# Constant tables loaded on the weight queue, and a final residual step in halves with stores on two queues

## The chip, the cores and the metric

The kernel runs on one core of a Trainium2 chip. The metric is the device time of one execution in microseconds (us), the median of several runs. PE is the matmul engine, PEld its weight loads, DVE the vector engine, ACT the scalar engine, POOL the general engine, SP the sync engine. SP and ACT each issue DMA transfers from a queue of their own (SPq and ACTq in the profile).

## The reference

A decoder trunk of two layers on 256 positions of width 2048 (float32): layer 0 is RetNet retention, layer 1 block attention, each followed by a gated MLP with a causal convolution, with RMS norms ahead of each part and at the end. Cut to what the change touches:

```python
def rms_norm(x, g):
    y = x * lax.rsqrt(jnp.mean(x * x, axis=-1, keepdims=True) + RMS_EPS)
    return y * g

def retention_mixer(h, w_in, gn_gain, w_out):
    q, k, v, g = split(h @ w_in)
    q = rotary(q, pos)                      # cos and sin tables: "rope"
    k = rotary(k, pos) * dk ** -0.5
    inner = (q @ k.T) * decay               # decay table per head: "dec"
    ...

def reference(x, ...):
    for i in range(2):
        h = h + mixer(rms_norm(h, mix_norm[i]))
        h = h + conv_ffn(rms_norm(h, ffn_norm[i]), ...)
    return rms_norm(h, final_norm)
```

## The kernel before

All weights are streamed once from memory in units of 1 MB (`raw`, three buffers). A unit has two halves; each half is split by ACT and DVE into a high part `wh` (L163) and a low part `wl` (L164), each in three buffers, and three products of high and low parts (or two instructions that cover them) give a float32-like result. `panel_b` (L277, L279) has the weights as the stationary operand, `panel_a` (L225 to L227) the activations. A list of halves is run in order (`run`); the split stands two halves ahead of the matmuls, and the load of unit u+1 is asked for at the split of unit u. A raw buffer is free again when both halves of its unit have been split.

The residual stream is `h` (two row tiles t of 128 positions, 2048 columns). At the start `first_dmas` loads pieces of x (into `h`) and of units 0 and 1 in turn on SP; `issue_dma` loads unit 2 in two pieces with the last two pieces of x ahead of them (L124 to L127), and later units whole (L129). `x_T` transposes x on PE (L301) into `hT`, four blocks of 128 columns at a time; the four blocks 4 to 7 need the x piece that L141 asks for. ACT's queue loads the identity and the gains first. `consts` (L518) loads the rotation table `rope` (256 KB) and the decay table `dec` (1 MB) on ACT's queue; it is asked for behind the third half (L526). The instructions on an engine need not stand in the order of these calls: the library that builds the program puts them in order, an engine then runs them strictly in that order, and a DMA is issued when the engine's queue comes to it. `rope` is first used in `use_rope` (L427), `dec` in `ret_scores` (L482).

At the end `last_half` (L610) handles the last 512 columns of each t when their matmuls are done: the residual addition from PSUM (L613), the squares with their sum (L614, which is L318 in the profile), the product with the final gain (L616), the sum of four partial sums of squares (`ssq`, L619), the power on POOL (L621), four multiplications by the result (L626 on ACT for j = 1, L628 on DVE for the others), and four stores on SP (L629). For t = 1 nothing is left on PE to run beside it.

Of the kernel before, what the change touches and what calls it, by code (L numbers as in the profile page):

```python
# [10 lines left out]
F32 = mybir.dt.float32  # L11
F32R = mybir.dt.float32r
BF16 = mybir.dt.bfloat16
AF = mybir.ActivationFunctionType
ALU = mybir.AluOpType
AX = mybir.AxisListType

P = 128
D = 2048
S = 256  # L20
# [48 lines left out]
def build(tc, a, out):  # L69
    nc = tc.nc  # L70
    ctx = ExitStack()
    cst = ctx.enter_context(tc.tile_pool(name="cst", bufs=1))
# [4 lines left out]
    scr = ctx.enter_context(tc.tile_pool(name="scr", bufs=1))  # L77
# [3 lines left out]
    act, dve, pe = nc.scalar, nc.vector, nc.tensor  # L81

    x = a["x"].rearrange("b (t p) d -> p (b t) d", p=P)
    o = out.rearrange("b (t p) d -> p (b t) d", p=P)

    ident = cst.tile([P, P], F32, name="ident")
    h = cst.tile([P, 2, D], F32, name="h")
# [5 lines left out]
    cw = [cst.tile([P, 4, 2 * NFB], F32, name=f"cw{i}") for i in range(2)]  # L93
    ones = cst.tile([P, P], F32, name="ones")
    mhalf = cst.tile([P, 2], F32, name="mhalf")
    ssq = cst.tile([P, 2, 4], F32, name="ssq")
    rB = cst.tile([P, S], F32, name="rB")
    rBq = cst.tile([P, S], F32, name="rBq")

# [11 lines left out]
    raws, parts = {}, {}  # L111

    order = []

    def load_x(c0, c1):
        nc.sync.dma_start(h[:, :, c0 * P : c1 * P], x[:, :, c0 * P : c1 * P])

    def issue_dma(u):
        src, n = units[u]
        raws[u] = wraw.tile([P, 2048], F32, name="raw")  # L120
        dst = raws[u].rearrange("p (c n) -> p c n", n=n)
        if u == 2:

            load_x(8, 12)  # L124
            nc.sync.dma_start(dst[:, :4], src[:, :4])
            load_x(12, 16)
            nc.sync.dma_start(dst[:, 4:], src[:, 4:])  # L127
        else:
            nc.sync.dma_start(dst, src)  # L129

    def first_dmas():
        (src0, n), (src1, _) = units[:2]
        for u in range(2):
            raws[u] = wraw.tile([P, 2048], F32, name="raw")
        dst0, dst1 = (raws[u].rearrange("p (c n) -> p c n", n=n) for u in range(2))
        load_x(0, 2)
        nc.sync.dma_start(dst0[:, :2], src0[:, :2])
        load_x(2, 4)
        nc.sync.dma_start(dst0[:, 2:4], src0[:, 2:4])
        nc.sync.dma_start(dst1[:, :4], src1[:, :4])  # L140
        load_x(4, 8)  # L141
        nc.sync.dma_start(dst0[:, 4:], src0[:, 4:])
        nc.sync.dma_start(dst1[:, 4:], src1[:, 4:])
        state["dma"] = 2

    def issue_split(i):
        u, hf = order[i]
        if i == 0:
            first_dmas()
        while state["dma"] <= min(u + 1, len(units) - 1):  # L150
            issue_dma(state["dma"])
            state["dma"] += 1
        r = raws[u][:, hf * 1024 : (hf + 1) * 1024]
        wh = whi.tile([P, 1024], F32R, name="wh")
        wl = wlo.tile([P, 1024], F32R, name="wl")
        if i == 0:
            for j in range(2):
                sl = slice(j * 512, (j + 1) * 512)
                x_T(2 * j, 2)
                act.activation(wh[:, sl], r[:, sl], AF.Copy)  # L160
                dve.tensor_tensor(wl[:, sl], r[:, sl], wh[:, sl].bitcast(F32), op=ALU.subtract)
        else:
            act.activation(wh, r, AF.Copy)  # L163
            dve.tensor_tensor(wl, r, wh.bitcast(F32), op=ALU.subtract)  # L164
        n = units[u][1]
        parts[i] = (wh.rearrange("p (c n) -> p c n", n=n), wl.rearrange("p (c n) -> p c n", n=n))
# [4 lines left out]
    def after(n, fn):  # L171
        later.append([state["mm"] + n, fn])
# [140 lines left out]
    def x_T(c0, n):  # L313
        to_T(hT, c0, lambda t, c: h[:, t, (c0 + c) * P : (c0 + c + 1) * P], c0, n)

    def square_t(j, t):
        junk = scr.tile([P, 512], BF16, name="junk")
        act.activation(junk, h[:, t, j * 512 : (j + 1) * 512], AF.Square, accum_out=ssq[:, t, j : j + 1])  # L318

    def square(j):  # L320
        for t in range(2):
            square_t(j, t)

    def rstd(dst, src, mul, eps):
        v = sml.tile([P, 2], F32, name="v")
        dve.tensor_scalar(v, src, mul, eps, op0=ALU.mult, op1=ALU.add)
        nc.gpsimd.tensor_tensor(dst, v, mhalf, op=ALU.pow)
# [2 lines left out]

    def make_r():
        v = sml.tile([P, 2], F32, name="vs")
        dve.reduce_sum(v, ssq, axis=AX.X)
        r["r"] = sml.tile([P, 2], F32, name="r")
        rstd(r["r"], v, 1.0 / D, RMS_EPS)

    def make_rB(use):
        make_r()
        pt = paux.tile([P, 2, S], F32, name="aux")
        for t in range(2):  # L340
            d = scr.tile([P, P], F32, name="diag")
            dve.tensor_scalar(d, ident, r["r"][:, t : t + 1], None, op0=ALU.mult)
            pe.matmul(pt[:, 0, t * P : (t + 1) * P], lhsT=ones, rhs=d, start=True, stop=True)  # L343
        use(pt[:, 0, :])
# [21 lines left out]
    dma0 = nc.scalar.dma_start  # L366
# [12 lines left out]
    def taps_load():  # L379
        for i in range(2):  # L380
            dma0(cw[i], a["l_taps"][:, i])
# [26 lines left out]
    def open_(name, **kw):  # L408
        es = ExitStack()
        pools[name] = es  # L410
        return es
# [3 lines left out]
    ret = {}  # L415
    yT = [None]

    def ret_open():
        es = open_("ret")
        p1 = es.enter_context(tc.tile_pool(name="ret1", bufs=1))  # L420
        ret["p1"] = p1
        ret["rope"] = p1.tile([P, 2, S], F32, name="rope")
        ret["dec"] = p1.tile([P, RH, S], F32, name="dec")
        yT[0] = p1.tile([P, 2 * KC, 2 * S], F32R, name="yT")
# [90 lines left out]
    xT_h = [hT]  # L515

    def ret_begin():
        def consts():  # L518
            dma0(ret["rope"], a["c_rope"])
            dma0(ret["dec"], a["c_decay"])  # L520

        for i in (1, 2, 3):
            midway[2 * i - 1] = lambda i=i: x_T(4 * i, 4)
        for j in range(4):
            after(1 + j if j < 2 else 2 * j, lambda j=j: square(j))
        after(3, lambda: consts())  # L526
        after(6, lambda: make_rB(use_rope))
        after(9, lambda: taps_load())

    def ret_head(hd):  # L530
        def k_done(acc):
            ret_qk("k")(acc)
            after(4, lambda: ret_scores(hd))

        def v_done(acc):
            ret_v(acc)
            after(2, lambda: ret_pv(hd))
            after(4, lambda: ret_yT(hd))
            if hd == 0:
                after(5, lambda: bias_load())  # L540
                after(7, lambda: bias_table())

        q = panel_b(w_in, hd * RDK, xT_h, ret_qk("q"), before=ret_begin if hd == 0 else None)
        k = panel_b(w_in, D + hd * RDK, xT_h, k_done)
        if hd == 0:
            emit_pairs(q, k)
        else:
            emit(q + k)
        emit(panel_a(w_in, KC, 4 * D + hd * RDV, xT_h, ret_g))
        emit(panel_a(w_in, KC, 2 * D + hd * RDV, xT_h, v_done))  # L550

    ret_open()
    for hd in range(RH):
        ret_head(hd)

# [54 lines left out]
    def last_half(acc, t):  # L610

        hs = h[:, t, 3 * 512 :]
        dve.tensor_tensor(hs, acc, hs, op=ALU.add)  # L613
        square_t(3, t)  # L614
        hg = ffn["p1"].tile([P, 512], F32, name=f"hg{t}", tag=f"u{t}")
        dve.tensor_tensor(hg, hs, fin[3], op=ALU.mult)  # L616
        v = sml.tile([P, 1], F32, name="vf")
        rf = sml.tile([P, 1], F32, name="rf")
        dve.reduce_sum(v, ssq[:, t, :], axis=AX.X)  # L619
        dve.tensor_scalar(v, v, 1.0 / D, RMS_EPS, op0=ALU.mult, op1=ALU.add)  # L620
        nc.gpsimd.tensor_tensor(rf, v, mhalf[:, :1], op=ALU.pow)  # L621
        for j in range(4):
            sl = slice(j * 512, (j + 1) * 512)
            src = h[:, t, sl] if j < 3 else hg
            if j == 1:
                act.activation(h[:, t, sl], src, AF.Copy, scale=rf)  # L626
            else:
                dve.tensor_scalar(h[:, t, sl], src, rf, None, op0=ALU.mult)  # L628
            nc.sync.dma_start(o[:, t, sl], h[:, t, sl])  # L629

    def ffn_layer(layer, begin, g_next, use_next, last):
        wu, wd = a["ffn_w_up"][layer], a["ffn_w_down"][layer]
# [180 lines left out]
```

## Time and profile before

| | us |
|---|---|
| median of 3 runs | 2618.73 |
| lowest and highest of them | 2617.67, 2626.54 |
| profiled execution, its own time | 2617.12 |
| span of the profiled execution | 2615.1 |
| PE busy in the span | 2596.3 |

The span runs from the first to the last instruction of the profiled execution; 2.0 us of its time lie around it. PE is busy for 99% of the span. What is left is read at the two ends: the first 15 us, where x and the first weights arrive, and the 8 us behind the last matmul.

### The profile page before, as it was taken

Reading aid. Unit: us, or ns where it says so; the run is one execution under the profiler, and the core shown is the slowest. Engines: PE = TensorE matmul, PEld = TensorE weight load, DVE = VectorE, ACT = ScalarE, POOL = GpSimd, SP = SyncE. Lnnn points to the kernel's source line nnn. Section 1 sums busy time; section 2 is a strip of 40 time slices with the busy share of each in tenths; the row PEclk is TensorE's granted clock in tenths of the full one; section 3 lists DMA queues with packets and bytes.
Section 4 is the critical chain, followed back from the end, with each engine's and each line's share of the span. In section 5 each row is a group of like instructions: output and inputs, shape, how many; then the busy total and the mean of one; then the engine's idle time right before and its main releaser. Section 6 shows DMA issues by size and latency. Waiting matters only on the chain.

```text
span 2615.1 us, 33467 instructions
## 1 busy us (share of the span) xinstructions
PE 2596.3 (99%) x13482; PEld 2223.3 (85%) x13482; DVE 1664.2 (64%) x2087; ACT 1300.7 (50%) x1659; POOL 10.2 (0%) x24
## 2 busy tenths in 40 slices
PE   8999999999999999999999999999999999999998
PEld 7888888888888888888888888888888888888887
DVE  5666566565557777777555566665577777775454
ACT  5444444444445555555444454444555555554443
POOL 0000000000000000000000000000000000000000
PEclk9999999999999999999999999999999999999999
DMA  7655555555555565556555555555565555556554
GB/s 238 227 187 178 181 170 186 178 190 180 193 181 189 193 193 187 187 191 193 193 192 188 196 189 181 174 185 174 180 193 189 187 189 193 193 187 207 194 193 153
DMA packets 372410, 493.85 MB, mean 189 GB/s; under 512 B 8080, under 2 KB 258976, under 8 KB 372000
## 3 DMA queue, kind: packets, MB, share of 16 engines
q1 hardware_dynamic: 366224, 482.38, 56.4%
q10 hardware_dynamic: 6032, 9.35, 1.1%
q8 instruction: 105, 1.72, 0.3%
q14 instruction: 49, 0.40, 0.0%
HBM read 489.57 MB, written 5.27 MB: 189 GB/s over the span
## 4 chain that ended last, share of the span: by engine, by line
PE 99%; DMA 0%; issue 0%; DVE 0%; ACT 0%; POOLq 0%; POOL 0%; DVEq 0%
PE acc L277 34%; PE acc L279 17%; PE acc L225 15%; PE acc L227 15%; PE acc L226 15%; PE aux L301 1%; PE aux L292 1%; PE aux L293 1%; PE aux L291 1%; DMA h<-in_x_dram 0%; PE aux L735 0%; PE aux L343 0%; DVE wl L164 0%; ACT wh L163 0%; DVE h L628 0%
## 5 line engine op out<-in xcount | busy, mean ns | idle before, releaser
L164 DVE TENSOR_TENSOR wl<-raw,wh 128x1024 fp32r<-128x1024 f32 x911 | 1115.2, 1225 | 880.5 <-ACT wh L163 879.8
L163 ACT ACTIVATE wh<-raw 128x1024 fp32r<-128x1024 f32 x911 | 966.2, 1061 | 1206.3 <-PE acc L227 589.5
L277 PE MATMUL acc<-hT,wh 128*128 128x512 f32 x3840 | 1343.3, 394 | 0.0
L279 PE MATMUL acc<-hT,wl 128*128 128x256 f32 x3840 | 1076.3, 280 | 0.0
L277 PEld LDWEIGHTS acc<-hT,wh 128*128 128x128 f32 x3840 | 719.6, 187 | 161.0
L279 PEld LDWEIGHTS acc<-hT,wl 128*128 128x128 f32 x3840 | 726.2, 189 | 1.0
L225 PE MATMUL acc<-wh,actT 128*128 128x512 f32 x704 | 274.0, 389 | 0.0
L227 PE MATMUL acc<-wh,actT 128*128 128x512 f32 x704 | 274.0, 389 | 0.0
L226 PE MATMUL acc<-wl,actT 128*128 128x512 f32 x704 | 273.9, 389 | 0.0
L225 PE MATMUL acc<-wh,hT 128*128 128x512 f32 x640 | 251.0, 392 | 0.1
L226 PE MATMUL acc<-wl,hT 128*128 128x512 f32 x640 | 249.4, 390 | 0.0
L227 PE MATMUL acc<-wh,hT 128*128 128x512 f32 x640 | 249.3, 390 | 0.0
L225 PEld LDWEIGHTS acc<-wh,actT 128*128 128x128 f32 x704 | 132.2, 188 | 27.7 <-DVE h L350 0.2
L227 PEld LDWEIGHTS acc<-wh,actT 128*128 128x128 f32 x704 | 132.2, 188 | 27.3
L226 PEld LDWEIGHTS acc<-wl,actT 128*128 128x128 f32 x704 | 132.2, 188 | 27.2
L586 DVE SCALAR_TENSOR_TENSOR t<-u,cw,t 128x256 f32<-128x256 f32 x352 | 146.8, 479 | 0.0
L227 PEld LDWEIGHTS acc<-wh,hT 128*128 128x128 f32 x640 | 120.2, 188 | 25.3
L225 PEld LDWEIGHTS acc<-wh,hT 128*128 128x128 f32 x640 | 120.2, 188 | 24.5 <-DVE bs L432 0.4
L226 PEld LDWEIGHTS acc<-wl,hT 128*128 128x128 f32 x640 | 120.3, 188 | 23.7
L225 PE MATMUL acc<-wh,yT 128*128 128x512 f32 x256 | 99.9, 390 | 0.0
L227 PE MATMUL acc<-wh,yT 128*128 128x512 f32 x256 | 99.6, 389 | 0.0
L226 PE MATMUL acc<-wl,yT 128*128 128x512 f32 x256 | 99.6, 389 | 0.0
(130 smaller groups left out, 1461.2 us busy)
## 6 DMA issues: line engine op xcount, KB each, us to landing
raw<-in_ffn_w_up_dram SPq DMA_DIRECT2D x176, 1024.0 KB, 5.1
raw<-in_ret_w_in_dram SPq DMA_DIRECT2D x93, 1024.0 KB, 5.2
raw<-in_ffn_w_down_dram SPq DMA_DIRECT2D x88, 1024.0 KB, 5.1
raw<-in_moba_w_qkv_dram SPq DMA_DIRECT2D x48, 1024.0 KB, 5.2
raw<-in_ret_w_out_dram SPq DMA_DIRECT2D x32, 1024.0 KB, 5.0
raw<-in_moba_w_out_dram SPq DMA_DIRECT2D x16, 1024.0 KB, 5.0
skewD<-tblD ACTq DMA_DIRECT2D x1, 3072.0 KB, 13.2
raw<-in_ret_w_in_dram SPq DMA_DIRECT2D x5, 512.0 KB, 9.3
```

The costliest lines, as they stand in the source:

```text
L163: act.activation(wh, r, AF.Copy)
L164: dve.tensor_tensor(wl, r, wh.bitcast(F32), op=ALU.subtract)
L225: pe.matmul(acc, lhsT=xh, rhs=wh[:, c, :], start=(k == 0), stop=False)
L226: pe.matmul(acc, lhsT=xh, rhs=wl[:, c, :], start=False, stop=False)
L227: pe.matmul(acc, lhsT=xl, rhs=wh[:, c, :], start=False, stop=(k == nk - 1))
L277: pe.matmul(acc[:, b, :], lhsT=wh[:, c, b * P : (b + 1) * P], rhs=xt[:, k, :], start=(k == 0), stop=False)
L279: pe.matmul(acc[:, b, S:], lhsT=wl[:, c, b * P : (b + 1) * P], rhs=xt[:, k, :S], start=False, stop=(k == KC - 1))
L291: pe.matmul(dst, lhsT=lh, rhs=rh, start=start, stop=False)
L292: pe.matmul(dst, lhsT=lh, rhs=rl, start=False, stop=False)
L293: pe.matmul(dst, lhsT=ll, rhs=rh, start=False, stop=stop)
L301: pe.transpose(pt[:, i, t * P : (t + 1) * P], src(t, c0 + i), ident)
L586: dve.scalar_tensor_tensor(t[:, i, :], u[:, i, tap : tap + S], c[:, tap, b : b + 1], t[:, i, :], op0=ALU.mult, op1=ALU.add)
```

## The change

The two loads of `consts` leave ACT's queue. `rope` is now issued on SP right behind the load of unit 3, `dec` right behind that of unit 5. In `last_half` the residual addition and the squares are made in two pieces of 256 columns each; the sums of squares of the two pieces have columns of their own, so `ssq` has five columns per t instead of four, and `make_r` reads the first four. The store of j = 1 goes to ACT's queue, the other three stay on SP.

```diff
-    ssq = cst.tile([P, 2, 4], F32, name="ssq")
+    ssq = cst.tile([P, 2, 5], F32, name="ssq")
...
+    consts = {}
...
             nc.sync.dma_start(dst, src)
+        if u in consts:
+            consts[u]()
...
-        dve.reduce_sum(v, ssq, axis=AX.X)
+        dve.reduce_sum(v, ssq[:, :, :4], axis=AX.X)
...
-        def consts():
-            dma0(ret["rope"], a["c_rope"])
-            dma0(ret["dec"], a["c_decay"])
...
-        after(3, lambda: consts())
...
     ret_open()
+    consts[3] = lambda: nc.sync.dma_start(ret["rope"], a["c_rope"])
+    consts[5] = lambda: nc.sync.dma_start(ret["dec"], a["c_decay"])
...
-        dve.tensor_tensor(hs, acc, hs, op=ALU.add)
-        square_t(3, t)
+        for i in range(2):
+            sl = slice(i * S, (i + 1) * S)
+            dve.tensor_tensor(hs[:, sl], acc[:, sl], hs[:, sl], op=ALU.add)
+            junk = scr.tile([P, 512], BF16, name="junk")
+            act.activation(junk[:, :S], hs[:, sl], AF.Square, accum_out=ssq[:, t, 3 + i : 4 + i])
...
-            nc.sync.dma_start(o[:, t, sl], h[:, t, sl])
+            (dma0 if j == 1 else nc.sync.dma_start)(o[:, t, sl], h[:, t, sl])
```

## Rows read from the trace of the kernel before

**Rows 1.** The page: the span, and busy us, share and instructions per engine.

```profile
span 2615.1 us, 33467 instructions
PE 2596.3 (99%) x13482; PEld 2223.3 (85%) x13482; DVE 1664.2 (64%) x2087; ACT 1300.7 (50%) x1659; POOL 10.2 (0%) x24
```

**Rows 2.** Stretches, PE alone: stretch, us, PE busy (instructions), clock, DMA share, GB/s.

```profile
60.00:2600.00 2540.00, 2540.00 (x13198) 1.00 0.58 188
2606.90:2615.10 8.20, 0.02 (x1) 0.72 0.67 249
```

**Rows 3.** The chain that ended last, first 20 us: start, us, what.

```profile
0.74 3.62 DMA h<-in_x_dram
4.37 8.69 DMA h<-in_x_dram
13.10 1.76 PE aux L301 x7
```

**Rows 4.** Timeline, ACT's queue: start, us, line, operation.

```profile
1.80 0.41 ACTq L519 DMA_DIRECT2D rope<-in_c_rope_dram  x1
4.20 0.34 ACTq L520 DMA_DIRECT2D dec<-in_c_decay_dram  x1
```

**Rows 5.** DMA issues by line: count, KB each, us from issue to landing.

```profile
dec<-in_c_decay_dram ACTq DMA_DIRECT2D x1, 1024.0 KB, 7.7
```

**Rows 6.** Stretches of 2 us, columns as in group 2.

```profile
4.00:6.00 2.00, 1.09 (x4) 1.00 0.90 312
8.00:10.00 2.00, 0.57 (x2) 1.00 1.05 420
12.00:14.00 2.00, 0.90 (x4) 1.00 1.06 357
```

**Rows 7.** Unit 3: its issue on SP, its landing, and the split on ACT.

```profile
16.93 0.37 SPq L129 DMA_DIRECT2D raw<-in_ret_w_in_dram  x1
DMA to landing us min/median/max: 7.8/7.8/7.8
26.19 1.05 ACT L163 ACTIVATE wh<-raw 128x1024 fp32r<-128x1024 f32 x1
```

**Rows 8.** Timeline, DVE: the first uses of the two tables.

```profile
36.09 0.68 DVE L427 TENSOR_TENSOR rope<-rope,aux 128x512 f32<-128x512 f32 x1
53.56 0.42 DVE L482 TENSOR_TENSOR pf<-aux,dec 128x256 f32<-128x256 f32 x1
```

**Rows 9.** Timeline behind the last matmul, DVE and ACT.

```profile
2606.96 0.69 DVE L613 TENSOR_TENSOR h<-acc,h 128x512 f32<-128x512 f32 x1 [0.31 <-PE acc L227]
2607.75 0.63 ACT L318 ACTIVATE junk<-h 128x512 bf16<-128x512 f32 x1 [1.65 <-DVE h L613]
2608.28 0.18 ACT L318 ACTIVATION_READ_ACCUMULATOR junk<-h 128x1 f32 x1
2609.51 0.72 ACT L626 ACTIVATE h<-h,rf 128x512 f32<-128x512 f32 x1 [1.04 <-POOL rf L621]
2610.31 0.48 DVE L628 TENSOR_SCALAR h<-hg,rf 128x512 f32<-128x512 f32 x1
```

**Rows 10.** Timeline, SP: the first and the last two of the last four stores.

```profile
2610.03 0.33 SPq L629 DMA_DIRECT2D out_dram<-h  x1
2610.93 0.89 SPq L629 DMA_DIRECT2D out_dram<-h  x2
```

**Rows 11.** Timeline: operations of 128x256 on DVE and ACT.

```profile
42.41 0.42 DVE L444 TENSOR_TENSOR m<-m,m 128x256 f32<-128x256 f32 x1
5.62 0.84 ACT L304 ACTIVATE hT<-aux,gains 128x256 fp32r<-128x256 f32 x2 [2.39 <-PE aux L301]
```

**Rows 12.** The page: matmuls of one line with other operand tiles, count, busy us, mean ns.

```profile
L225 PE MATMUL acc<-wh,actT 128*128 128x512 f32 x704 | 274.0, 389 | 0.0
L225 PE MATMUL acc<-wh,hT 128*128 128x512 f32 x640 | 251.0, 392 | 0.1
```

**Rows 13.** The chain near the end, one step of the matmuls.

```profile
2600.12 0.23 PE acc L225
```

## The prediction

> **What bounds the kernel now.** I read the busy times first: PE works 2596.3 of the 2615.1 us [rows 1], so 18.8 us are idle. Next the stretches, to see where they lie: from 60 to 2600 us PE is never idle, and 8.2 us stand behind the last matmul [rows 2]. The rest, some 10.6 us, is the start. The change touches no matmul and no split, so it can gain only there, at most 18.8 us, and never all of it, since the first data must come and the last must go.
>
> Then the chain of waits at the start [rows 3]. It names one transfer: the piece of x for blocks 4 to 7, issued at 4.37 and landed at 13.06. PE waits for it until 13.10, transposes it, and from there has work until the end. So that landing sets the end of the whole kernel less the tail. The chain also shows that this issue at 4.37 came just as the first piece of x landed (0.74 + 3.62 = 4.36).
>
> What does this piece share the DMA engines with? ACT's queue issued rope at 1.80 and dec at 4.20 [rows 4], long before the calls' place in the code (behind the third half): the builder moved them forward. dec lands at 4.20 + 7.7 = 11.9 [rows 5], 1.2 us before the piece. The engines are full in this time: 312 to 420 GB/s with a busy share of 0.90 and above [rows 6]. So both tables, 1280 KB or 1.31 million bytes, are moved ahead of the piece that PE waits for.
>
> **The tables.** The change takes these 1.31 million bytes out from in front. At 420 GB/s, the rate while dec was moving, they took 3.1 us; at 357, the rate when SP alone was feeding, 3.7 us [rows 6]. The nearer row is hard to choose: the rate with dec in flight is the rate at which dec went, but what is left behind goes at SP's own. I take 3.4, so that the piece lands near 9.7. The lower bound is that SP alone ramps more slowly than both queues did: if the 5.3 us from the first piece's landing at 4.4 to 9.7 went at the 312 GB/s of the stretch from 4 to 6 us, not at the mean of the other two stretches, 389, they would take 1.3 us more. The gain lies between 2.1 and 3.7.
>
> The Trainium skill, "DMA: Bandwidth & Descriptors", section Specifications, gives some 358 GB/s as what HBM yields to one core. By that the tables would be worth 3.7 us and the sum would be 0.3 us lower. The trace went above it, at 420 GB/s over 2 us [rows 6], so the measured rate keeps its place.
>
> Does PE start 3.4 us sooner? The other loads of the start are on the same queue, behind or just ahead, and come forward by the same bytes, and the splits follow them. I count nothing for the matmuls' slow first steps: PE is idle ahead of them in either case.
>
> **Where the tables go.** On SP they stand among the weight loads: two more issues of 0.37 us [rows 7], on a queue that issues one unit about every five us; hidden. What they can delay is a unit behind them. Unit 3 was issued at 16.93 and landed 7.8 us later, at 24.7; its split ran at 26.19 [rows 7]. In the code rope stands behind unit 3, but as the builder moved it before, it may put rope, or both, ahead of unit 3, because that load waits for a buffer and the tables wait for nothing. With both ahead, unit 3 lands where it did, at 24.7, while its split could run at 22.8: up to 1.9 us late, part of which the split's lead of two halves takes up. Cost 0 as called, 0 to 1.9 otherwise; I take 0, since rope alone costs 0.7 us of transfer and the old margin was 1.5. The tables' users: rope at 36.09, dec at 53.56 on DVE [rows 8], some 33 and 50 after the shift. Had they come late, DVE, which runs in order, would hold the wl splits behind them, and PE behind those. rope lands near 22 and dec, behind unit 5, in the middle thirties at the latest: margins of 10 us.
>
> **The tail, squares.** Before, the addition starts at 2606.96 and takes 0.69, the square starts 0.10 behind its end, its sum is read 0.53 later and takes 0.18: done 1.50 after the start [rows 9]. In halves: the first addition ends at 0.42 [rows 11], the first square starts at 0.52. A square of 256 columns, from the operation of that size on ACT (0.42 each) [rows 11], hands over to the read of its sum after some 0.32; then 0.18 for the read, 0.03 to the next: the second square starts at 1.05 (its addition is done by 0.85), its sum is read from 1.37 and done at 1.55 to 1.57. That is 0.07 later than before: the second read of a sum eats what the overlap gives. Bounds: 0.2 us sooner, if the two squares overlapped fully, 0.3 later. The gain product (L616) moves by as little and hides beside the squares. For t = 0 the same happens beside matmuls and costs nothing.
>
> **The tail, stores.** Four stores on SP begin at 2610.03 and the last ends its issue at 2611.82, 0.43 to 0.47 each [rows 10]. The data of the last is ready at 2610.79 [rows 9], so SP's issuing is late, not the data. With three on SP, beginning 0.07 later: 2610.10, 2610.53, 2611.00, done 2611.40. ACT's multiplication ends at 2610.23 [rows 9], so its store is issued by some 2610.8, before SP's last. The 3.3 us from the last issue to the span's end stay. Net of both tail edits -0.4; bounds -0.7 to +0.3 (nothing, if what lands last isn't the last issued, with the squares' worst). For t = 0, ACT's store issue ends before ACT's next square; nothing waits.
>
> **The sum.** 2617.12 of the profiled execution, less 3.4, less 0.4: 2613.3. The median of the runs stands 1.6 above that execution, so the same sum on the median is 2614.9. I forecast 2614.2 between them. Against 2618.73 that is 0.17% faster, within the 0.5% that a measurement of this kernel can tell from no change.
>
> **The rivals.**
> The tables still stand in front. If the builder moves them on SP ahead of the x pieces, the piece for blocks 4 to 7 lands as before, and only the tail's 0.4 is left: 2616.7, on the median's footing 2618.3. For it: rope did move ahead by three halves. Against it: the x pieces wait for nothing either and were called first. 8%.
>
> Half of the gain is held elsewhere: unit 3 late by up to 1.9 us, or the splits on ACT and DVE become the chain. 2617.12 - 1.5 - 0.4 = 2615.2. For it: the margin of 1.5 us [rows 7]. 12%.
>
> More is gained: in the gap of PE ahead of 13.10 there could be matmuls of the first half, if the builder orders them ahead of the transposes. Up to 2 us more: 2611.3. 8%.
>
> Slower: ssq grows from 32 to 40 bytes in each partition, and tiles allocated behind it may lie at other addresses. If a matmul's read of 512 columns then touched one more memory line of four float32 columns, at 0.23 us for 512 columns [rows 13] that is 1.8 ns for each of 13482 matmuls [rows 1], 24 us in all: 2613.3 + 24.3 = 2638. It decides from 0.28 ns per matmul on, which eats the 3.8 us. Against it: matmuls of one line that read actT and hT, which lie at different places, take 389 and 392 ns [rows 12]; the trace shows no addresses, so those two may share an alignment. 4%. The Trainium skill, "SBUF — State Buffer", section Specifications (TRN2), speaks for this rival: it says that the memory has lines of 16 bytes and that each crossing to a new line costs. No row of this trace shows such a price.
>
> **How the numbers follow.** The forecast has 68%: startup 2.1 to 3.7, tail -0.7 to +0.3, on either footing 2612.7 to 2616.9. The range goes below to the case of more gain and above to that of no gain at the start on the median's footing, with part of the scatter of the runs: 2610.8 to 2619.2. Faster by over 0.5% would take 13 us out of 18.8 idle: 1%. Slower by over 0.5% comes only from the moved tiles: 3%. Else the same: 96%.
>
> **What would show it.** Right: the chain's transfer of x lands near 9.7 instead of 13.06, PE's transposes start there, PE is idle some 3.4 us less and has no new gap up to 60 us; behind the last matmul there are two reads of sums and the power on POOL starts no sooner; SP issues three stores and ends some 0.4 us nearer to the last matmul, and ACT's store is issued in between. Wrong: rope or dec issued before the second piece of unit 2, a wait of ACT for unit 3, or a matmul mean that moved by a nanosecond or more.

## The result: 0.76% slower, and where the time went

| | before | after |
|---|---|---|
| median of 5 runs, us | 2618.40 | 2639.49 |
| lowest and highest, us | 2617.67, 2626.54 | 2639.45, 2641.22 |
| profiled execution, own time, us | 2617.12 | 2639.49 |
| its span, us | 2615.1 | 2637.7 |

The ratio is 1.0076, 95% interval 1.0062 to 1.0090. The forecast was 2614.2 (2610.8 to 2619.2), so the result lies outside the range, at the rival that had 4%. Some executions of the kernel before, and of those that place their tiles like it, run one stretch of the up projections at 236 ns per `wh` matmul instead of 230, 9 us more in all (2627 instead of 2618); where a profile below is such an execution, the text says so.

Lines of the code have moved: L277 and L279 are now L280 and L282, L225 to L227 are L228 to L230, L129 is L130, L301 is L304, L613 is L615, the squares of the tail (L318) are L617, L621 is L624 and L629 is L632.

The page of the kernel after, busy times (against [rows 1]):

```profile
span 2637.7 us, 33475 instructions
...
PE 2623.5 (99%) x13482; PEld 2225.6 (84%) x13482; DVE 1665.7 (63%) x2089; ACT 1301.5 (49%) x1663; POOL 10.2 (0%) x24
```

PE is busy 27.2 us longer with the same 13,482 matmuls, and idle 14.2 us instead of 18.8. So the change won 4.6 us of idle time, as it was meant to, and lost 27.2 us inside the matmuls.

The steady stretch of the kernel after, PE alone (columns as in [rows 2]):

```profile
60.00:2600.00 2540.00, 2540.00 (x13079) 1.00 0.57 187
```

PE has no gap here in either kernel and the granted clock is 1.00 in both, but 119 fewer matmuls fit in than in [rows 2]. At 0.227 us each (a step of the kind in [rows 13]) these are 27.0 us.

Which matmuls grew (line, operands, count, busy us, mean ns of one): first two groups of the kernel before, then the page of the kernel after.

```profile
L277 PE MATMUL acc<-hT,wh 128*128 128x512 f32 x3840 | 1343.3, 394 | 0.0
L279 PE MATMUL acc<-hT,wl 128*128 128x256 f32 x3840 | 1076.3, 280 | 0.0
```

```profile
L280 PE MATMUL acc<-hT,wh 128*128 128x512 f32 x3840 | 1359.8, 397 | 0.0
L282 PE MATMUL acc<-hT,wl 128*128 128x256 f32 x3840 | 1080.9, 281 | 0.0
...
L228 PE MATMUL acc<-wh,actT 128*128 128x512 f32 x704 | 274.1, 390 | 0.0
...
L228 PE MATMUL acc<-wh,hT 128*128 128x512 f32 x640 | 254.2, 397 | 0.1
...
L228 PE MATMUL acc<-wh,yT 128*128 128x512 f32 x256 | 99.9, 390 | 0.0
```

In [rows 12] `wh,actT` stood at 389 and `wh,hT` at 392. Now every group that reads `hT` is longer, and no other by more than 1 ns: `hT,wh` went from 394 to 397, `hT,wl` from 280 to 281, `wh,hT` from 392 to 397. These means include the overlap of one matmul with the next; what counts is the step from start to start. The timeline of PE around 2000 us (start, us, what), first before:

```profile
2000.13 0.39 PE L277 MATMUL acc<-hT,wh 128*128 128x512 f32 x1
2000.36 0.28 PE L279 MATMUL acc<-hT,wl 128*128 128x256 f32 x1
2000.48 0.39 PE L277 MATMUL acc<-hT,wh 128*128 128x512 f32 x1
2000.71 0.28 PE L279 MATMUL acc<-hT,wl 128*128 128x256 f32 x1
2000.83 0.39 PE L277 MATMUL acc<-hT,wh 128*128 128x512 f32 x1
```

and after:

```profile
2000.04 0.40 PE L280 MATMUL acc<-hT,wh 128*128 128x512 f32 x1
2000.28 0.28 PE L282 MATMUL acc<-hT,wl 128*128 128x256 f32 x1
2000.40 0.39 PE L280 MATMUL acc<-hT,wh 128*128 128x512 f32 x1
2000.63 0.28 PE L282 MATMUL acc<-hT,wl 128*128 128x256 f32 x1
2000.74 0.40 PE L280 MATMUL acc<-hT,wh 128*128 128x512 f32 x1
```

Before, the step behind a `wh` matmul is 0.23; after, it alternates 0.24 and 0.23. Worked out from all start times of the up projections, it grew from 230 to 234.6 ns, and the one behind `wl` from 116.7 to 118.7; in `panel_a` the steps that read `hT` grew from 227 to 233.5, and those that read `actT` or `yT` stayed at 227.

Aligning the two traces matmul by matmul gives the account. (The first 141 stand in another order, so up to there the matmuls are only counted.) At the 50th matmul the kernel after is 4.80 us ahead, from there to the last it loses 27.34, and the tail adds under 0.1. Together 22.6, the difference of the spans. The two up projections of the MLPs are 18.5 of the 27.3: each takes 482.0 us before and 491.2 after.

**Where the tiles lie.** The program as built gives the start of every tile in the partition, in bytes. In it a tile takes a multiple of 32 bytes, so `ssq` takes 32 before (4 x 2 floats) and 64 after (5 x 2 floats, 40 bytes), and every tile allocated behind it moves by 32.

| tile | before | after |
|---|---|---|
| hT | 33472 | 33472 |
| wh | 96704 | 96736 |
| wl | 108992 | 109024 |
| actT, oT (one place) | 123584 | 123616 |
| yT | 133824 | 133856 |

Before, any two of these differ by a multiple of 256 bytes (wh less hT is 63232, 247 times 256; actT less wh is 26880, 105 times). After, `hT` alone is 32 off from the others, and the matmuls that grew are those with `hT`.

### The profile page after: what moved, and what is told of

Its sections match the earlier page's. It is cut to its first block, busy times and chain, and to the rows that moved or that the text cites. A ratio compares the mean times of both kernels' runs of the same rounds, so it can differ in the third digit from the quotient of the medians.

```text
span 2637.7 us, 33475 instructions
## 1 busy us (share of the span) xinstructions
PE 2623.5 (99%) x13482; PEld 2225.6 (84%) x13482; DVE 1665.7 (63%) x2089; ACT 1301.5 (49%) x1663; POOL 10.2 (0%) x24
## 4 chain that ended last, share of the span: by engine, by line
PE 99%; DMA 0%; issue 0%; DVE 0%; ACT 0%; SPq 0%; POOLq 0%; POOL 0%; DVEq 0%
PE acc L280 34%; PE acc L282 17%; PE acc L228 15%; PE acc L229 15%; PE acc L230 15%; PE aux L304 1%; PE aux L296 1%; PE aux L295 1%; PE aux L294 1%; DMA h<-in_x_dram 0%; PE aux L738 0%; PE aux L346 0%; DVE wl L167 0%; ACT wh L166 0%; ACT junk L617 0%
## 5 line engine op out<-in xcount | busy, mean ns | idle before, releaser
L280 PE MATMUL acc<-hT,wh 128*128 128x512 f32 x3840 | 1359.8, 397 | 0.0
L282 PE MATMUL acc<-hT,wl 128*128 128x256 f32 x3840 | 1080.9, 281 | 0.0
L280 PEld LDWEIGHTS acc<-hT,wh 128*128 128x128 f32 x3840 | 721.7, 188 | 174.5 <-DVE hT L310 0.2
L282 PEld LDWEIGHTS acc<-hT,wl 128*128 128x128 f32 x3840 | 724.6, 189 | 1.0
L228 PE MATMUL acc<-wh,actT 128*128 128x512 f32 x704 | 274.1, 390 | 0.0
L230 PE MATMUL acc<-wh,actT 128*128 128x512 f32 x704 | 273.9, 389 | 0.0
L228 PE MATMUL acc<-wh,hT 128*128 128x512 f32 x640 | 254.2, 397 | 0.1
L230 PE MATMUL acc<-wh,hT 128*128 128x512 f32 x640 | 252.6, 395 | 0.0
L228 PEld LDWEIGHTS acc<-wh,actT 128*128 128x128 f32 x704 | 132.2, 188 | 27.6 <-DVE h L353 0.2
L230 PEld LDWEIGHTS acc<-wh,actT 128*128 128x128 f32 x704 | 132.2, 188 | 27.5
L229 PEld LDWEIGHTS acc<-wl,actT 128*128 128x128 f32 x704 | 132.2, 188 | 27.3
L230 PEld LDWEIGHTS acc<-wh,hT 128*128 128x128 f32 x640 | 120.0, 187 | 29.2
L228 PEld LDWEIGHTS acc<-wh,hT 128*128 128x128 f32 x640 | 120.0, 188 | 28.1 <-DVE bs L435 0.4
L228 PE MATMUL acc<-wh,yT 128*128 128x512 f32 x256 | 99.9, 390 | 0.0
L230 PE MATMUL acc<-wh,yT 128*128 128x512 f32 x256 | 99.7, 389 | 0.0
```

Source lines behind the costliest of these rows:

```text
L228: pe.matmul(acc, lhsT=xh, rhs=wh[:, c, :], start=(k == 0), stop=False)
L229: pe.matmul(acc, lhsT=xh, rhs=wl[:, c, :], start=False, stop=False)
L230: pe.matmul(acc, lhsT=xl, rhs=wh[:, c, :], start=False, stop=(k == nk - 1))
L280: pe.matmul(acc[:, b, :], lhsT=wh[:, c, b * P : (b + 1) * P], rhs=xt[:, k, :], start=(k == 0), stop=False)
L282: pe.matmul(acc[:, b, S:], lhsT=wl[:, c, b * P : (b + 1) * P], rhs=xt[:, k, :S], start=False, stop=(k == KC - 1))
```

## Experiments: does the place of the tiles cost the 27 us?

The first theory is that the time follows from where a matmul's operands lie relative to each other. The rivals are that the 27 us come from the moved loads, or from the code of the tail. "Steady" below is what a kernel loses against the one before between the 50th and the last matmul, from traces aligned as above.

**e1.** The kernel before, with 32 unused bytes behind `ssq`; no instruction differs.

```diff
     ssq = cst.tile([P, 2, 4], F32, name="ssq")
+    cst.tile([P, 8], F32, name="pad0")
```

> The kernel before, with an unused tile of 32 bytes behind ssq, so that all tiles behind it (raw, wh, wl, actT and the rest, not hT) lie 32 bytes higher; no instruction is other than before. Theory P (the place of the weight parts against hT is what the matmuls pay for): steps of the matmuls with hT grow as in the changed kernel, 27 us in all, 2645 us. Rival Q (the other order of loads, the halves or the two queues slow it): 2618 us, as before. Rival C (the place makes no difference): 2618 us.

Measured: 2645.05 against 2618.36, ratio 1.0097 (1.0079 to 1.0115); steady +27.33, where the kernel after had +27.34. Its matmuls by line:

```profile
L277 PE MATMUL acc<-hT,wh 128*128 128x512 f32 x3840 | 1359.3, 397 | 0.0
L279 PE MATMUL acc<-hT,wl 128*128 128x256 f32 x3840 | 1080.7, 281 | 0.0
```

The same 397 and 281 as after. An unused tile costs the whole loss.

**e3.** The kernel after, its `mhalf` and `ssq` in one tile of 64 bytes, so that all else lies as before.

```diff
-    mhalf = cst.tile([P, 2], F32, name="mhalf")
-    ssq = cst.tile([P, 2, 5], F32, name="ssq")
+    misc = cst.tile([P, 16], F32, name="misc"); mhalf = misc[:, 10:12]
+    ssq = misc[:, :10].rearrange("p (t j) -> p t j", t=2)
```

> The changed kernel with mhalf and ssq in one tile of 64 bytes, so that every tile behind them lies where it lay in the kernel before. All instructions of the change are there. Theory P: 2618.4 less the 4.8 us by which the matmuls of the changed kernel start sooner, 2613 to 2614 us, steps of the matmuls with hT as before. Rival Q: 2639 us.

Measured: 2612.87 against 2618.36, ratio 0.9986 (0.9971 to 1.0001). At the 50th matmul it is 4.70 us ahead, and 0.1 is lost from there to the 8000th; behind that its profiled execution (2621.62) is one at 236 ns. All that the change does, without the 32 bytes, is worth 5.5 us by the medians, which the interval, with executions at both levels in it, can't tell from no change; the aligned trace shows the 4.7. The 32 bytes cost 26.6 (2639.49 less 2612.87).

**e4.** The kernel before, with an unused tile ahead of `hT` grown by 32 bytes, so that all operands move together.

```diff
-    cst.tile([P, 16], F32, name="gap0")
+    cst.tile([P, 24], F32, name="gap0")
```

> The kernel before with the unused tile ahead of hT 32 bytes larger, so that hT and all behind it lie 32 bytes higher together. Theory P in its relative form (hT against wh and wl): no change, 2618 us. Its absolute form (wh, wl at a place that is no multiple of 64 bytes): 2645 us, and then the matmuls with actT would be slower too, which they were not in the changed kernel.

Measured: 2616.12 against 2618.36, ratio 0.9984 (0.9972 to 0.9996); steady -1.9, the `hT,wh` group 393. It is the place of the operands relative to each other that costs; this one move of all together was worth 2 us, in the other direction. One of its ten executions took 3705.29 us, for which nothing here gives a reason; the others took 2615.3 to 2616.7.

**e2, e10, e9.** How the cost depends on the distance. e2 is the kernel after with 32 bytes more (64 in all); e10 and e9 are the kernel before with 128 and 256 unused bytes behind `ssq`.

```diff
+    cst.tile([P, 8], F32, name="pad0")      # e2, on the kernel after
...
+    cst.tile([P, 32], F32, name="pad0")     # e10
...
+    cst.tile([P, 64], F32, name="pad0")     # e9
```

> The changed kernel with 32 unused bytes more behind ssq, so that all behind it lies 64 bytes higher than in the kernel before. Theory P: if the pattern repeats with 64 bytes, the 27 us go and the gain of the start stays, 2612 us; if it repeats with more, something between 2612 and 2640. Rival Q: 2639 us, as the changed kernel.

> The kernel before, with 128 unused bytes behind ssq. 0 and 256 bytes gave 2618 us, 32 gave 2645, 64 gave 17 us over what the start and tail leave. If the pattern repeats with 128 bytes: 2618. If 256 is the period and half of it is as far as one can be from it: over 2630.

> The kernel before, with 256 unused bytes behind ssq. In the kernel before the places of hT and of wh, wl, actT, yT and oT differ by whole multiples of 256 bytes; 32 bytes off cost 27 us, 64 bytes off 22 us. If the pattern repeats with 256 bytes (or fewer, down to 128): 2618 us. If it needs more: over 2630 us.

| distance added, bytes | ratio, interval | steady, us | ns of hT,wh / hT,wl / wh,hT |
|---|---|---|---|
| 0 (before) | 1 | 0 | 394 / 280 / 392 |
| 32 (e1) | 1.0097 (1.0079 to 1.0115) | +27.3 | 397 / 281 / 397 |
| 64 (e2) | 1.0058 (1.0040 to 1.0076) | +22.3 | 398 / 281 / 393 |
| 128 (e10) | 1.0076 (1.0061 to 1.0091) | +20.0 | 395 / 283 / 397 |
| 256 (e9) | 0.9998 (0.9989 to 1.0008) | 0.0 | 394 / 280 / 392 |

e2 has the start's gain of the change in its ratio, the others have not. A period of 64 or of 128 bytes falls; 256 brings the time back. At the distances tried below it (none lies between 128 and 256) the cost is 20 to 27 us, and it moves between the kinds of matmul. The Trainium skill, "SBUF — State Buffer", section Specifications (TRN2), says that the memory has lines of 16 bytes and that each crossing to a new line costs. Shifts of 32, 64 and 128 bytes are whole lines and change no crossing, and they cost 27, 22 and 20 us: the measurement shows another effect than that rule.

**e5.** The kernel before, with `actT`, `oT` and `yT` moved by 32 bytes, and `hT`, `wh`, `wl` left.

```diff
     scr = ctx.enter_context(tc.tile_pool(name="scr", bufs=1))
+    scr.tile([P, 8], F32, name="pad0")
```

> The kernel before, with 32 unused bytes behind wl: hT, wh and wl lie where they lay, while actT, yT and oT, the other operands of the matmuls with wh and wl, lie 32 bytes higher. Theory P (it is the place of one operand against the other): now the matmuls with hT keep their steps and those with actT, yT and oT, 3264 of 128x512 in panel_a, go from 227 to 233 or so: 2618.4 + 3264 x 6.5 ns = 2639.6 us. Rival H (something is particular to hT or to its neighbours): 2618 us.

Measured: 2638.05 against 2618.13, ratio 1.0076 (1.0059 to 1.0093); steady +20.1. Its matmuls by line:

```profile
L277 PE MATMUL acc<-hT,wh 128*128 128x512 f32 x3840 | 1343.3, 394 | 0.0
...
L225 PE MATMUL acc<-wh,actT 128*128 128x512 f32 x704 | 278.5, 396 | 0.0
...
L225 PE MATMUL acc<-wh,hT 128*128 128x512 f32 x640 | 250.9, 392 | 0.1
```

Now the `hT` groups stay at 394 and 392, and `actT` goes from 389 to 396 (its step from 227 to 233.3 ns). The cost went to the pairs whose distance changed. So no tile is special; the distance is.

**e6 and e15: which two reads meet?** While a matmul streams its moving operand, the stationary operand of the next one is loaded (PEld is busy for 84% of the span beside PE's 99%). In `panel_b`, `hT` streams, and `wh` and `wl` are loaded in turn. Either the matmul's own two operands matter, or the stream and the load of the *next* weights. e6 moves `wl` and all behind it by 32; e15 moves `wh` alone by 32, and what lies behind it by 256.

```diff
+    ctx.enter_context(tc.tile_pool(name="padp", bufs=1)).tile([P, 8], F32, name="pad0")    # e6
     wlo = ctx.enter_context(tc.tile_pool(name="wlo", bufs=3))
...
+    ctx.enter_context(tc.tile_pool(name="pada", bufs=1)).tile([P, 8], F32, name="pad0")    # e15
     whi = ctx.enter_context(tc.tile_pool(name="whi", bufs=3))
+    ctx.enter_context(tc.tile_pool(name="padb", bufs=1)).tile([P, 56], F32, name="pad1")   # e15
     wlo = ctx.enter_context(tc.tile_pool(name="wlo", bufs=3))
```

> The kernel before, with 32 unused bytes between wh and wl: hT and wh lie where they lay, wl and all behind it 32 bytes higher. While one matmul streams its columns the weights of the next are loaded. Theory N (the streamed operand meets the load of the next weights): in panel_b the matmul with wh has the load of wl beside it and gets slower, the one with wl has the load of wh beside it and keeps its 117 ns. Theory O (a matmul's own two operands): the other way round, the step of the matmul with wl grows. Either way some 2630 to 2650 us; without an effect, 2618.

> The kernel before with wh 32 bytes higher, and wl and all behind it 256 bytes higher, so that only wh is off the common place; the mirror image of the run in which only wl and what lies behind it was. Theory N (the streamed operand meets the load of the next weights): in the second layer's up projection the step of the matmul with wl, which has the load of wh beside it, grows from 117 to 119 or more, and that of the matmul with wh stays near 230 or falls. Theory O (a matmul's own two operands): the step of the matmul with wh grows to 234 or more, that with wl stays at 117. Median by either some 2625 to 2645 us.

Measured: e6 2641.59 against 2618.13, ratio 1.0090 (1.0075 to 1.0105), steady +23.3; e15 2650.51 against 2626.95 (the kernel before ran mostly at 236 ns in that set), ratio 1.0095 (1.0077 to 1.0113), steady +34.6.

The two theories were to be told apart by the steps in the up projections. In e6 the step behind a `wh` matmul grew from 230 to 232 ns, and the one behind `wl` fell from 116.7 to 115. That is no cost: a pair takes 347 ns as before, only the start of the `wl` matmul in it has moved. The number of matmuls in 400 us of an up projection says the same (columns as in [rows 2]; in order, the kernel before, e6, e15 and the kernel after):

```profile
1950.00:2350.00 400.00, 400.00 (x2310) 1.00 0.59 190
1950.00:2350.00 400.00, 400.00 (x2310) 1.00 0.58 190
1950.00:2350.00 400.00, 400.00 (x2280) 1.00 0.57 188
1950.00:2350.00 400.00, 400.00 (x2266) 1.00 0.58 187
```

So with `wl` alone off from `hT` the up projections lose nothing, though either theory named a matmul that should pay. The cost of e6 lies in `panel_a` (28 us, while the other stretches of `panel_b` are 5 faster): with `actT`, `oT` and `yT`, which are off from `wh` there, and also with `hT`, off from `wl` alone, whose mean step grew from 227.3 to 231.8 ns. In e15 `wh`'s step grew to 234 and `wl`'s to 117.5, 4.4 ns for a pair: `wh` was moved, and its own matmul pays, which speaks for the own operands. Neither theory fits both runs, so which reads meet stays open. That distance decides is shown; the mechanism is not.

## Experiments: the start and the tail

**e8.** The change without its part on the squares, and with `ssq` as before: only the tables and the ACT store.

```diff
+    consts[3] = lambda: nc.sync.dma_start(ret["rope"], a["c_rope"])
+    consts[5] = lambda: nc.sync.dma_start(ret["dec"], a["c_decay"])
...
+            (dma0 if j == 1 else nc.sync.dma_start)(o[:, t, sl], h[:, t, sl])
```

> The changed kernel without the halves of the last addition and squares, and with ssq as before, so that nothing lies elsewhere: the tables on SP and the store of j = 1 on ACT are left of the change. From the start 4.8 us less than before; from the stores nothing if the end is set by the bytes of the four stores (1 MB at some 380 GB/s behind the first one's issue), 0.4 less if it is set by SP's issues. So 2613.5 us by the first and 2613.1 by the second, read in the profile from the last matmul's start to the end of the span: 8.6 or 8.2 us.

Measured: median 2612.65 against 2618.13, 5.5 us less; the ratio over all runs, those at 236 ns too, is 0.9993 (0.9978 to 1.0009), which takes in no change. (Two of the ten took 2621.13 and 2622.55, one 2630.75, 18 us more than the median, as two stretches at 236 would.) Aligned, it is 4.70 ahead at the 50th matmul and 4.68 at the last. From the last matmul's start to the end it took 8.55 us, so of the two expectations for the stores it is the one by their bytes (8.6, not 8.2). What PE waited for in the first 60 us (us in all, times, longest), before:

```profile
PE aux L301 <- DMA h<-in_x_dram: 10.5, 3, 4.5
```

and in e8, where the kernel after has the same 5.9 in 2 waits:

```profile
PE aux L304 <- DMA h<-in_x_dram: 5.9, 2, 4.5
```

The third wait is gone altogether: 4.6 us. The forecast had 3.4, by an earlier landing alone. The timeline of PE in the kernel after shows what else changed:

```profile
7.03 1.11 PE L304 MATMUL aux<-ident,h 128*128 128x128 f32 x4 [1.41 <-DMA h<-in_x_dram]
7.80 0.77 PE L280 MATMUL acc<-hT,wh 128*128 128x512 f32 x1
8.37 0.41 PE L282 MATMUL acc<-hT,wl 128*128 128x256 f32 x1
...
12.44 0.27 PE L304 MATMUL aux<-ident,h 128*128 128x128 f32 x1
...
13.71 0.93 PE L304 MATMUL aux<-ident,h 128*128 128x128 f32 x7
```

The builder put the matmuls of the first half ahead of the transposes of blocks 4 to 7, so PE has work from 7.8 us on while that piece is under way. In [rows 3] the transposes came first and PE stood until 13.10. Is it the bytes or the order?

**e12.** e8 with the old order forced: the transposes of blocks 4 to 7 come behind the first matmul.

```diff
+                        if state["mm"] == 0 and c == 0 and b == 0:
+                            x_T(4, 4); es.enter_context(tc.issue_after(state["tr"].ins))
...
-        for i in (1, 2, 3):
+        for i in (2, 3):
```

> The tables on SP and the store on ACT's queue, no halves, nothing lies elsewhere, and the transposes of blocks 4 to 7 are held behind the first matmul as in the kernel before. Their piece of x landed at 13.06 before and at 10.8 in the changed kernel. Theory B: PE waits for it until 10.8, 2.3 us less than before, 2615.8 us. Theory O: the order is the old one, so no gain, 2618.

Measured: 2615.84 against 2617.87, 2.0 us less; ratio 0.9995 (0.9986 to 1.0005). PE's waits in its first 60 us:

```profile
PE aux L308 <- DMA h<-in_x_dram: 8.5, 3, 4.5
```

So 10.5, 8.5 and 5.9: in PE's waits the bytes alone give 2.0, the order on top of them 2.6. Of the 2.0 the aligned traces keep 1.2 at the last matmul: in e12 four pairs of steps behind the transposes still take 0.64 us each instead of 0.35, before two did. By the medians it is 2.0 and 3.4, but the interval of e12 takes in no change. So the bytes alone are worth 1.2 to 2.0, and the order with them the larger part of the 4.7.

**e11.** The order alone: the kernel before, tables in front as they were, the transposes of blocks 4 to 7 held behind the matmuls.

```diff
-                        midway[state["mm"]]()
+                        with tc.issue_after(box["last"].ins): midway[state["mm"]]()
```

> The kernel before, both tables in front as they were, but the transposes of blocks 4 to 7 are held behind the matmuls of the first half and a half, as they stand in the changed kernel; before, they stood behind the first matmul, and PE waited there for their piece of x. Theory O (the other order on PE gives the gain at the start): the first half runs while the tables land, the next needs its low part at 14.15, so some 3.5 us of the 4.8: 2614.6 us. Theory B (the bytes that no longer stand in front give it): at most 1 us, 2617 to 2618.

Measured: 2620.29 against 2617.87, ratio 1.0009 (0.9999 to 1.0018): nothing won; the 2.4 lost by the medians can't be told from no change. Its PE at the start (this profile is one at 236 ns, which begins far behind these rows):

```profile
10.74 0.63 PE L277 MATMUL acc<-hT,wh 128*128 128x512 f32 x1
13.10 0.50 PE L277 MATMUL acc<-hT,wh 128*128 128x512 f32 x1 [1.73 <-ACT wh L163]
```

It begins its matmuls at 8.03, much as the kernel after does, but with the tables in front the next weights are late and PE stops for the split; later it waits for `hT` (the weight loads of L277 stand 4.5 us for it in the first 40). By 20 us PE has been idle 0.9 us less than before, by 40 us 1.3 more. With e12 this shows that in these two forms neither the bytes nor the order gives the 4.6 us alone: the new order fills the gap, and with the tables away the weights arrive in time to keep it filled. It isn't shown that no order could win without the bytes, since the builder moved work on ACT in e11 too.

**e13.** Do the last bytes or the last issues set the end? The kernel before, where the stores of t = 1 move half of the columns (the other half of these rows is left out of the output).

```diff
+            sl = sl if t == 0 else slice(j * 512, j * 512 + 256)
             nc.sync.dma_start(o[:, t, sl], h[:, t, sl])
```

> The kernel before, which for t = 1 stores only half of the columns of each of its four stores (the other half of that part of the output is left out): as many issues, half of the bytes. If the tail is set by the bytes of the four stores: 0.5 MB less at some 380 GB/s, the span ends 1.4 us sooner behind the last matmul's start, 7.2 instead of 8.6. If it is set by the issues on SP: 8.6 as before.

Measured, one run: 2616.4; from the last matmul's start to the end 7.73 us instead of 8.58 (8.5 to 8.6 in every other profile of this document). The four issues are unchanged; half the bytes make the end 0.85 earlier. So the bytes set the end before; with half of them the last stores land 0.48 us apart, as they are issued, and the issues set it. The kernel after, its stores in stretches of 1 us (the last two columns are the DMA share and GB/s; PEclk stands ahead of them):

```profile
2633.00:2634.00 1.00, 0.00 (x0) 0.00 (x0) 0.33 (x1) 0.00 (x0) 0.00 (x0) 0.50 0.61 227
2634.00:2635.00 1.00, 0.00 (x0) 0.00 (x0) 0.00 (x0) 0.00 (x0) 0.00 (x0) 0.50 1.01 373
2635.00:2636.00 1.00, 0.00 (x0) 0.00 (x0) 0.00 (x0) 0.00 (x0) 0.00 (x0) 0.50 1.03 389
2636.00:2637.00 1.00, 0.00 (x0) 0.00 (x0) 0.00 (x0) 0.00 (x0) 0.00 (x0) 0.50 0.16 59
```

The transfers start in the first of these stretches and are full for the two that follow, share 1.01 and 1.03. In the kernel before they were as full (389 and 373 GB/s, share 1.04 and 1.01).

**e14.** e8 with 256 bytes of padding: the version to keep, with the table loads and the ACT store, without the halves, and with operands a multiple of 256 apart.

> The tables on SP and the store of j = 1 on ACT's queue, no halves, and 256 unused bytes behind ssq. Theory P with a period of 256 bytes: 2612.7 us, as without the unused bytes. Without that period: over 2630.

Measured: 2621.15 against 2626.95 in that set of runs, ratio 0.9972 (0.9957 to 0.9988). Both kernels showed both levels here: 2612.7 to 2614.0 against 2618.3 to 2618.6, and 2621.2 to 2621.9 against 2626.7 to 2628.0. At either it is more than 4 us ahead of the kernel before, so it beats both kernels, though by under half a per cent of the kernel before.

## Why the prediction was wrong, step by step

**The failed step: "ssq grows".** I had the mechanism among the rivals, with its place (the moved tiles), its price (1.8 ns for each matmul, 24 us) and its time (2638; measured 2637.7 for the span, 2639.49 for the time). I gave it 4%, for one reason: that `actT` and `hT` lie at different places and cost alike, 389 and 392 [rows 12]. That reason was empty, and I had half said so ("those two may share an alignment"): all operands lay at multiples of 256 bytes from each other, so the two groups were one case and not two. The trace of before could not show it; the built program's tile addresses could have. The right reading was that [rows 12] give no evidence, and then the rival needs a larger chance. So the sum put the matmuls' steps at no change ("The change touches no matmul and no split"), and the runs showed 27.3 us there. My mechanism for the rival (one more memory line touched) was also not the one: a pad of 256 bytes, no less moved, costs nothing (e9), and moving all together costs nothing (e4). That its 24 us came near 27.3 was luck: it charged all 13,482 matmuls 1.8 ns each, and those that read `hT` paid 2 to 6 and the others nothing.

**The tables: right in kind, short in size.** The piece of x was to land near 9.7 instead of 13.06. Its issue was at 4.63, not 4.37, and took 6.2 us: 10.8. Part of the cause stands on ACT's queue of the kernel after:

```profile
1.80 0.93 ACTq L384 DMA_DIRECT2D cw<-in_l_taps_dram  x2
```

Two loads of 176 KB moved up into the place of `rope` [rows 4]; at the 420 GB/s of [rows 6] they are 0.86 us, by my estimate; no run took them away. So the landing moved by 2.2, near the lower bound of 2.1, and e12's waits give 2.0 for it. The rest, 2.6, is the rival "more is gained", matmuls of the first half in PE's gap, up to 2 us, 8%: it is what happened, and e11 did not get it without the bytes. "I count nothing for the matmuls' slow first steps" was not right either for the order that I assumed: in e12 more of them were slow, and they took back part of the 2.0.

**The tables' new place: right.** `rope` is issued behind unit 3, `dec` behind unit 4 (not 5), on SP:

```profile
15.46 0.37 SPq L130 DMA_DIRECT2D raw<-in_ret_w_in_dram  x1
15.87 0.58 SPq L551 DMA_DIRECT2D rope<-in_c_rope_dram  x1
17.38 0.37 SPq L130 DMA_DIRECT2D raw<-in_ret_w_in_dram  x1
17.79 0.66 SPq L552 DMA_DIRECT2D dec<-in_c_decay_dram  x1
```

They land 7.4 and 12.0 us later, at 23.3 and 29.8, and are used at 31.6 and 49.2. Nothing waits for them, and neither table went ahead of the x pieces.

**The squares: right.** The tail of the kernel after on ACT, where the additions start at 2629.50:

```profile
2629.96 0.42 ACT L617 ACTIVATE junk<-h 128x256 bf16<-128x256 f32 x1 [1.26 <-DVE h L615]
2630.28 0.19 ACT L617 ACTIVATION_READ_ACCUMULATOR junk<-h 128x1 f32 x1
2630.50 0.42 ACT L617 ACTIVATE junk<-h 128x256 bf16<-128x256 f32 x1
2630.82 0.19 ACT L617 ACTIVATION_READ_ACCUMULATOR junk<-h 128x1 f32 x1
```

The second sum is read at 2631.01, 1.51 behind the additions' start, against 1.50 before [rows 9] and 1.55 to 1.57 forecast. The second read of a sum does eat the overlap, and the power on POOL starts 2.39 behind the last matmul's start in both kernels.

**The stores: the issue was right, its worth was not.** The last store on SP in the kernel after:

```profile
2633.47 0.42 SPq L632 DMA_DIRECT2D out_dram<-h  x1
```

It ends 4.82 behind the last matmul's start instead of 5.29: 0.47 sooner, where 0.42 was forecast. But the span ends at 8.6 in both. "SP's issuing is late, not the data" was the failed step: the four stores move 1.05 MB, and at the 373 to 389 GB/s shown above these need 2.7 to 2.8 us whoever issues them. No gain lay within my bounds, but under another condition ("nothing, if what lands last isn't the last issued"): the last one issued still landed last, 3.3 us behind its issue instead of 2.8. The Trainium skill, "DMA: Bandwidth & Descriptors", section Rules for kernel authors, says that spreading DMAs over several issuing engines saves issue time only and gives no bandwidth; by that rule the term would have been zero. The trace agrees: 0.47 less issuing, the end unmoved.

**The account.** The forecast's sum for the profiled execution was 2613.3. Add 27.3 for the tiles, take 1.4 for the start (4.8 instead of 3.4), add 0.4 for the tail that gave nothing: 2639.6, measured 2639.49.

## What to carry to other kernels

A few bytes more in a small tile allocated early move every tile behind it; where matmuls fill the span, look up where their operands lie before and after, and keep hot operands at a distance that has been timed (here a multiple of 256 bytes), with a pad if need be. Two groups that cost the same are evidence against a cause only if the cause differs between them. Behind the last operation count bytes as well as issues, and of a load taken away from the front expect both: that others move up into its place, and that the order of the waiting engine's own work changes.

## What the runs showed that I had not expected

- A matmul's step depends on the distance of its operands in the partition: 227 ns at multiples of 256 bytes, 233.3 to 233.5 at 32 bytes more, in `panel_a` (after, e5). The clock granted was 1.00 in either.
- The cost is back at nothing at 256 bytes and isn't even below that: 27.3, 22.3 and 20.0 us at 32, 64 and 128 bytes.
- At the best distance some executions still run one stretch of up projections at 236 ns instead of 230. Such a stretch takes 491.2 us instead of 482.0 (the second one in e3's profile), just what each takes with the tiles 32 bytes off. So the good distance allows the faster step and doesn't ensure it. What decides stays open.
